# The last two gate blocks and W_out's rows move under the last memory unit, and the band attention's row sums are divided out on Pool

## The chip, the core and the metric

One core of a Trainium2 chip runs one launch of the kernel. The metric is the device time of that launch in microseconds (us), lower is better. The engines are PE (TensorE, matmuls; PEld is its weight load), DVE (VectorE), ACT (ScalarE), POOL (GpSimd) and SP, whose queue issues every DMA here.

## What is computed

One step of a one-layer encoder with 1024 prompt tokens and 8 running streams of 16 tokens, so 1152 tokens of width 1024. Cut to what matters:

```python
aq, ak, av, bq, bk, bv, mq, gate = split_projection(x, w_in, pos)   # x @ w_in, 3584 columns; b_q, b_k rotated
o_a = band_attention(aq, ak, av, a_rel_bias)     # 4 heads x 64: own chunk of 64 tokens and 8 before
o_b = diff_post(diff_attention(bq, bk, bv, lam)) # 4 heads x 128, two softmax maps
o_m = memory_attention(mq, mk, mv)               # 4 heads x 64 into 256 memory tokens
mixed = concatenate([o_a, o_b, o_m], -1)         # 1024 wide
y = (mixed * silu(gate)) @ w_out
out = layer_norm(2 ** 0.25 * x + y, ln_g, ln_b)
```

All arithmetic is in 32 bits. The new keys and values are outputs too.

## The kernel before

**Products.** An operand is split into a rounded high part and the rest (`hi`, `lo`), and a product is three matmuls, hi by hi, lo by hi, hi by lo. `w_in` is taken in 28 blocks of 128 output features; 8 of them are gate blocks, one for each 128 of the mixing width. x lies in SBUF transposed, as `xh`, `xl`, in three parts c = 0, 1, 2 of 384 tokens. `chunk` (L317 on) makes one block for one part: 8 steps over the depth of 3 matmuls each (L146 to L148), 24 matmuls of 384 columns into a `pp` tile of PSUM, of which there are two. `load_next` (L134) brings a weight block in two halves (raw tile `wraw`, two of them, L142), rounds each on ACT into `whi` (L130) and takes the difference on Pool into `wlo` (L131). Gate results go through ACT (L434) and DVE (L435) to a DRAM scratch `gates` (L436).

**Units.** The attention is done in eight units, `ORD`: M0, B0 to B3, A0, A1, M1 (two heads, or one of B). `main` is the unit's attention in small steps (scores L448 and L449, exponential, transposes L461, their split on ACT and DVE, products L663), and `merge` lays `fill` between them: the v block of the unit, gate blocks, the q block of the next unit. `NG` says how many gate blocks go with each unit; its first entry is done at the very start, part by part beside M0's q block. Results of a unit go to a DRAM scratch `mixed`.

**Band units (A).** `score` of `attention_a` takes the scores of 128 tokens against up to 640 keys, adds the bias and finds the extreme on DVE (L697), exponentiates on ACT (L703) and divides by the row sums in `normalise`: a reciprocal (L525) and a multiplication (L530), both on DVE.

**The end.** W_out has 1024 rows in 8 blocks k. `load_wout(c)` brings three of them (two for c = 2) into the room of x's part c, so it can write there only when every block has used that part. Each row block comes in two halves of 128x512 through the same two `wraw` tiles (L1084); ACT rounds each (L1085), DVE takes the rest of the first half and Pool of the second (L1086). An out step t (128 tokens) needs `mixed(t)`: gates and unit results read back (L985, L987), combined on DVE (L990, L998, L1001), split (L995 on ACT, L996 on DVE); then 48 matmuls of 512 columns over k (L1031), the residual and the layer norm. `out_steps` makes t = 0 and 1 as the fill of M1; its last step k = 7 needs the first quarter of M1's result (`closed`). Steps t = 2 to 8 follow M1 on their own, and M1's part for the running streams lies among them (its first products on PE are L790).

**Order.** A scheduler puts the instructions of each engine in order by priorities and its own time line when the kernel is built, so the written order is not the executed one. Each engine, and SP's queue, then runs strictly in that order: an instruction that waits holds all behind it.

Of the kernel before, what the change touches and what calls it, by code (L numbers as in the profile page):

```python
# [10 lines left out]
ALU = mybir.AluOpType  # L11
# [27 lines left out]
LW = 1  # L39
LEAD = 4.25  # L40
ORD = ["M0", "B0", "B1", "B2", "B3", "A0", "A1", "M1"]
NG = [1, 1, 1, 1, 1, 1, 2, 0]
GW = 2
PE = mybir.EngineType.PE
SP = mybir.EngineType.SP
# [17 lines left out]
def hybrid_step(tc, d, o):  # L63
    nc = tc.nc
# [50 lines left out]
    order = [base[names[0][0]][0] + names[0][1]]  # L115
    gates = iter(GATES)
    for i, (kind, idx) in enumerate(names):
        order += [b + idx for b in base[kind][1:]]
        late = [20 + next(gates) for _ in range(NG[i])]
        if i != 6:  # L120
            order += late
        if i < 7:
            order.append(base[names[i + 1][0]][0] + names[i + 1][1])
        if i == 6:
            order += late
    loaded = {}

    def split_half(hi, lo, raw, i, eng):
# [4 lines left out]
    def load_next(early=None):  # L133
        if len(loaded) == len(order):  # L134
            return
        blk = order[len(loaded)]
        hi = wst.tile([P, KT, P], F32R, tag="whi")
        lo = wst.tile([P, KT, P], F32R, tag="wlo")
        loaded[blk] = (hi, lo)
        for i in range(2):  # L140
            raw = early.tile([P, 4, P], F32, tag="mraw", bufs=MB) if early else wst.tile([P, 4, P], F32, tag="wraw")
            nc.sync.dma_start(raw, d["win"][blk, :, 512 * i : 512 * i + 512].rearrange("p (k c) -> p k c", c=P))  # L142
            split_half(hi, lo, raw, i, nc.gpsimd)
# [52 lines left out]
    with tc.tile_pool(name="early", bufs=1) as ep_:  # L196
        ep = Pool(ep_)
        memh = ep.tile([P, KT, 256], F32R, tag="memh")
        meml = ep.tile([P, KT, 256], F32R, tag="meml")
        wm = []  # L200

        def split_part(hi, lo, raw, a, b, eng):
            nc.scalar.copy(hi[:, a:b], raw)
            eng.tensor_tensor(out=lo[:, a:b], in0=raw, in1=f(hi[:, a:b]), op=ALU.subtract)  # L204

        def load_mem_w(blk):
            if blk < 2:
                hi, lo = [op_.tile([P, KT, P], F32R, tag=f"qa{i}", bufs=2) for i in range(2)]
            else:
                if blk == 2:  # L210
                    hi, lo = [op_.tile([P, KT, P], F32R, tag=f"ka{i}") for i in range(2)]
                else:
                    both = op_.tile([P, 2, KT, P], F32R, tag="va")
                    hi, lo = both[:, 0], both[:, 1]
            wm.append((hi, lo))
            cut = PC if blk == 0 else [0, 4, 8]
            for i, (a, b) in enumerate(zip(cut, cut[1:])):
                raw = ep.tile([P, b - a, P], F32, tag="mraw", bufs=MB)
                nc.sync.dma_start(raw, d["wmem"][blk, :, P * a : P * b].rearrange("p (k c) -> p k c", c=P))
                split_part(hi, lo, raw, a, b, nc.gpsimd if i or blk == 0 else nc.vector)  # L220
                if blk == 0:
                    memr = ep.tile([P, b - a, 256], F32, tag="xr", bufs=XB)
                    nc.sync.dma_start(memr, d["memT"][:, 256 * a : 256 * b].rearrange("p (k c) -> p k c", c=256))
                    split_part(memh, meml, memr, a, b, nc.vector)

        def load_x(c):
            for a in range(0, KT, 2):
                xr = ep.tile([P, 2, CH], F32, tag="xr", bufs=XB)
                nc.sync.dma_start(xr, d["xT"][c, :, CH * a : CH * (a + 2)].rearrange("p (k c) -> p k c", c=CH))
                split_part(xh[c], xl[c], xr, a, a + 2, nc.gpsimd if a in XP else nc.vector)  # L230

        kvs = []

        def mem_block(blk):
            ps = ps_p.tile([P, 256], F32, tag="pp")
            for k in range(KT):
                step(ps, wm[blk], memh, meml, k)
            kv = ep.tile([P, 256], F32, tag=f"memkv{blk}")
            kvs.append(kv)
            nc.vector.tensor_copy(kv, ps)  # L240


        warm = ps_t.tile([P, P], F32, tag="pt")
        for _ in range(WU):
            nc.tensor.matmul(warm, lhsT=sqzs[0][0], rhs=sqzs[0][0], start=True, stop=True)
        stores = []
        mem0 = []

        def mem_part(blk):
            mem_block(blk)  # L250
            out, scr = (o["mkT"], mkscr) if blk < 2 else (o["mvT"], mvscr)
            stores.append((out[blk % 2], kvs[blk]))
            if blk == 1:
                stores.append((mkscr, kvs[blk]))
            if blk < 2:
                return
            pt = ps_t.tile([P, 2, P], F32, tag="pt")
            for t in range(2):
                nc.tensor.transpose(pt[:, t], kvs[blk][:, t * P : (t + 1) * P], ident)
            mv = ep.tile([P, 2, P], F32, tag=f"memv{blk}")  # L260
            nc.scalar.copy(mv, pt)
            if blk == 3:
                stores.append((mvscr.rearrange("p (t e) -> p t e", t=2), mv))
            else:
                mem0.append(mv)

        with tc.manual_schedule(engines={SP}):
            for blk in range(4):
                load_mem_w(blk)
            load_next(ep)  # L270
            load_x(0)
            for blk in range(4):
                mem_part(blk)
            load_next(ep)
            load_x(1)
            load_x(2)
            for out, kv in stores:
                nc.sync.dma_start(out, kv)
            nc.sync.dma_start(cos, d["cos"])
            nc.sync.dma_start(sin, d["sin"])  # L280
        units = [setup(*n) for n in names]
        split_mem(units[0], kvs[0], mem0[0].rearrange("p t (h e) -> p t h e", h=2))
# [11 lines left out]
    for i in range(2):  # L294
        nc.vector.tensor_tensor(
            out=dl[:, i * 128 : i * 128 + 64], in0=dl[:, i * 128 : i * 128 + 64],
# [226 lines left out]
    def normalise(e, r, act):  # L523

        nc.vector.reciprocal(r, r)  # L525
        if act:
            nc.vector.tensor_scalar_mul(r, r, 0.5)
            nc.scalar.mul(e, e, r)
        else:
            nc.vector.tensor_scalar(out=e, in0=e, scalar1=r, scalar2=0.5, op0=ALU.mult, op1=ALU.mult)  # L530
# [134 lines left out]
    def attention_a(u, need):  # L665
# [3 lines left out]
        def unit(j, h):  # L669
# [14 lines left out]
            def score(i):  # L684
                kt0 = base[i]
                n = (i - kt0 + 1) * P
                b0 = 640 - n
                w_ = n if n <= 512 else n // 2
                e = pp.tile([P, 640], F32, tag="p")
                p[i] = e  # L690
                nm = small.tile([P, 2], F32, tag="nm")
                low = 3e38
                for c in range(n // w_):
                    ps = ps_s.tile([P, 512], F32, tag="ps")
                    cs = slice(c * w_, (c + 1) * w_)
                    scores(u, h, i, ps[:, 0:w_], kt0 * P + c * w_, w_)
                    nc.vector.tensor_tensor_reduce(  # L697
                        out=e[:, cs], in0=ps[:, 0:w_], in1=u.nb[:, h, b0 + c * w_ : b0 + (c + 1) * w_],
                        scale=1.0, scalar=low, op0=ALU.add, op1=ALU.min, accum_out=nm[:, c : c + 1])
                    low = nm[:, c : c + 1]  # L700
                nm = low
                rs = small.tile([P, 1], F32, tag="rs")
                nc.scalar.activation(e[:, :n], e[:, :n], AF.Exp, bias=nm, scale=-1.0, accum_out=rs)  # L703
                normalise(e[:, :n], rs, False)
                if i == 0:
                    nc.gpsimd.memset(e[:, P : 2 * P], 0.0)

# [249 lines left out]
    gates = iter(GATES)  # L957
# [166 lines left out]
    for i, u in enumerate(units):  # L1124
# [12 lines left out]
            vb, ve = [], []  # L1137
        more = []
        gs = [gate_block(next(gates)) for _ in range(NG[i] if i else 0)]
        if i != 6:  # L1140
            more += sum(sum(gs, []), [])
        if nxt:
            more += sum(q_of(nxt), [])
            fill = vb + more[:4] + ve + more[4:]
            if i == 6:

                for c in range(3):
                    for g in gs:
                        fill += g[c]
                    fill.append((0.0, lambda c=c: load_wout(c)))  # L1150
                stages = sample_of(u)
                fill = fill[:ES] + with_stages(fill[ES:], EV)
            if u.kind == "M":
                fill = with_stages(fill, 8)
        else:
            fill = out_steps(0, u) + out_steps(1, u)

        def need(kt, u=u, fill=fill):
            while u.vdone <= kt // 3:
# [105 lines left out]
```

## Time and profile before

| | us |
|---|---|
| median of 3 runs | 701.17 (700.27 to 702.02) |
| the profiled execution | 702.39, of which the span of its trace is 700.6 |
| PE busy | 669.1 (96%) |
| DVE busy | 483.8 (69%) |
| ACT busy | 354.0 (51%) |
| POOL busy | 211.9 (30%) |

A busy PE is not PE at its peak: matmuls overlap, so the distance between two starts, not the length of one, is what a matmul costs, and idle time of PE counts only waits that are longer than that overlap. A lowered clock shows as a granted clock (PEclk) under 1.00.

### The profile page before, as it was taken

What the parts mean: (1) busy time and instruction counts of PE and PEld (TensorE: products, weight loads), DVE (VectorE), ACT (ScalarE), POOL (GpSimd) and SP (SyncE); (2) the same over time, 40 slices, a digit from 0 to 9 for tenths busy, and PEclk for the clock granted to TensorE, in tenths of its full rate; (3) what the DMA queues carried; (4) which work ended last, traced back from release to release, by engine and by line L of the source; (5) the groups of instructions that cost most, each with busy time, mean ns of one, the idle gap of its engine ahead of it and who ended that gap; (6) DMA issues with size and microseconds to landing.
All of it is one profiled execution on the core that took longest, in us unless ns stands there. A gap on an engine that the chain in (4) does not pass through costs nothing.

```text
span 700.6 us, 12139 instructions
## 1 busy us (share of the span) xinstructions
PE 669.1 (96%) x4306; PEld 620.0 (88%) x4306; DVE 483.8 (69%) x1201; ACT 354.0 (51%) x922; POOL 211.9 (30%) x250
## 2 busy tenths in 40 slices
PE   8989999999999999999999999999999795999995
PEld 7989899999989999999999999999999573787884
DVE  4858766789676866798566627764785749388954
ACT  5747555457455654465455635675565654121000
POOL 7843322352235323442233222111022200224102
PEclk9999999999999999999999999999999797999998
DMA  8851342213221223133222122132236505776311
GB/s 260 304 182 52 124 132 78 53 50 106 84 72 38 97 72 84 38 99 132 87 69 68 50 91 73 40 138 72 88 109 180 171 7 186 268 270 208 139 72 61
DMA packets 55692, 78.90 MB, mean 113 GB/s; under 512 B 9368, under 2 KB 33232, under 8 KB 55632
## 3 DMA queue, kind: packets, MB, share of 16 engines
q1 hardware_dynamic: 55632, 78.13, 33.9%
q8 instruction: 34, 0.56, 0.3%
q14 instruction: 26, 0.21, 0.1%
HBM read 57.69 MB, written 20.42 MB: 111 GB/s over the span
## 4 chain that ended last, share of the span: by engine, by line
PE 83%; DMA 5%; DVE 5%; ACT 3%; POOL 1%; issue 1%; SPq 0%; POOLq 0%; ACTq 0%; DVEq 0%
PE pp L146 16%; PE pp L147 16%; PE pp L148 16%; PE pp L1031 7%; PE ps L1031 6%; PE pt L461 4%; PE po L624 4%; PE ps L449 4%; PE ps L448 4%; PE po L663 3%; DMA wraw<-in_wout 2%; DVE xl L204 1%; PE pt L875 1%; DMA p<-mixed 1%; PE ps L790 1%
## 5 line engine op out<-in xcount | busy, mean ns | idle before, releaser
L146 PE MATMUL pp<-xh,whi 128*128 128x384 f32 x672 | 229.8, 342 | 3.3 <-DVE qa L163 2.5
L148 PE MATMUL pp<-xh,wlo 128*128 128x384 f32 x672 | 228.8, 340 | 0.3 <-POOL wlo L131 0.3
L147 PE MATMUL pp<-xl,whi 128*128 128x384 f32 x672 | 228.9, 341 | 0.0
L146 PEld LDWEIGHTS pp<-xh,whi 128*128 128x128 f32 x672 | 126.5, 188 | 6.6 <-issue 2.7
L147 PEld LDWEIGHTS pp<-xl,whi 128*128 128x128 f32 x672 | 126.5, 188 | 2.7 <-POOL xl L204 0.4
L148 PEld LDWEIGHTS pp<-xh,wlo 128*128 128x128 f32 x672 | 126.4, 188 | 1.8 <-POOL wlo L131 0.6
L131 POOL TENSOR_TENSOR wlo<-wraw,whi 128x512 fp32r<-128x512 f32 x52 | 70.5, 1376 | 110.7 <-ACT whi L130 104.0
L590 ACT ACTIVATE p<-ps,nm 128x512 f32<-128x512 f32 (+3 forms) x96 | 55.3, 580 | 39.8 <-DVE nm L587 26.5
L448 PE MATMUL ps<-ka,qa 128*128 128x512 f32 (+4 forms) x176 | 59.3, 343 | 4.7 <-ACT p L752 4.1
L461 PE MATMUL pt<-ident,p 128*128 128x128 f32 x332 | 56.0, 281 | 2.4 <-DVE ptl L465 1.0
L449 PE MATMUL ps<-kl,qa 128*128 128x512 f32 (+4 forms) x176 | 57.7, 331 | 0.0
L585 DVE TENSOR_REDUCE nm<-ps 128x1 f32<-128x512 f32 (+3 forms) x96 | 51.3, 549 | 7.1 <-PE ps L449 5.5
L465 DVE TENSOR_TENSOR ptl<-pt,pth 128x512 fp32r<-128x512 f32 x56 | 38.3, 686 | 15.5 <-ACT pth L464 15.3
L461 PEld LDWEIGHTS pt<-ident,p 128*128 128x128 f32 x332 | 40.6, 144 | 5.9 <-DVE ptl L465 1.4
L464 ACT CAST pth<-pt 128x512 fp32r<-128x512 f32 x56 | 32.9, 587 | 17.8 <-PE pt L461 15.3
L1031 PE MATMUL pp<-xh,whi 128*128 128x512 f32 (+1 forms) x96 | 38.0, 395 | 3.1 <-ACT whi L995 3.1
L448 PEld LDWEIGHTS ps<-ka,qa 128*128 128x128 f32 x176 | 33.7, 192 | 6.9 <-ACT p L752 5.5
L1031 PE MATMUL pp<-xl,whi 128*128 128x512 f32 (+1 forms) x96 | 37.3, 388 | 0.0
L1031 PE MATMUL pp<-xh,wlo 128*128 128x512 f32 (+1 forms) x96 | 36.4, 385 | 0.0
L624 PE MATMUL po<-pth,va 128*128 128x256 f32 (+1 forms) x160 | 35.0, 282 | 0.0
L449 PEld LDWEIGHTS ps<-kl,qa 128*128 128x128 f32 x176 | 33.9, 193 | 0.3
L161 POOL TENSOR_TENSOR qa<-t,qa 64x384 fp32r<-64x384 f32 (+1 forms) x24 | 22.0, 918 | 38.1 <-ACT qa L159 37.1
(223 smaller groups left out, 1322.2 us busy)
## 6 DMA issues: line engine op xcount, KB each, us to landing
wraw<-in_win SPq DMA_DIRECT2D x52, 256.0 KB, 2.8
xr<-in_xT SPq DMA_DIRECT2D x12, 384.0 KB, 5.8
gates<-t SPq DMA_DIRECT2D x24, 192.0 KB, 2.7
qa<-in_xn SPq DMA_DIRECT2D x9, 512.0 KB, 3.5
wraw<-in_wout SPq DMA_DIRECT2D x16, 256.0 KB, 4.4
p<-gates SPq DMA_DIRECT2D x8, 512.0 KB, 5.7
out_y<-qa SPq DMA_DIRECT2D x16, 256.0 KB, 2.0
mixed<-od SPq DMA_DIRECT2D x28, 128.0 KB, 1.8
```

What stands on the lines that cost most here:

```text
L131: eng.tensor_tensor(out=lo[:, h], in0=raw, in1=f(hi[:, h]), op=ALU.subtract)
L146: nc.tensor.matmul(ps, lhsT=w[0][:, k], rhs=xh_[:, k], start=(k == 0), stop=False)
L147: nc.tensor.matmul(ps, lhsT=w[0][:, k], rhs=xl_[:, k], start=False, stop=False)
L148: nc.tensor.matmul(ps, lhsT=w[1][:, k], rhs=xh_[:, k], start=False, stop=(k == KT - 1))
L448: nc.tensor.matmul(ps, lhsT=u.qa[h][:, qs], rhs=u.ka[h][:, k0 : k0 + n], start=True, stop=False)
L449: nc.tensor.matmul(ps, lhsT=u.qa[h][:, qs], rhs=kl[h][:, k0 : k0 + n], start=False, stop=True)
L461: nc.tensor.transpose(pt[:, t, q * P : (q + 1) * P], p[q][:, cols[t][q] : cols[t][q] + P], ident)
L465: nc.vector.tensor_tensor(out=lo, in0=pt, in1=f(hi), op=ALU.subtract)
L585: nc.vector.tensor_reduce(out=nm[:, m, c : c + 1], in_=ps[c][:, : b - a], axis=AX.X, op=ALU.max, negate=True)
L590: nc.scalar.activation(e[:, a:b], ps[c][:, : b - a], AF.Exp, bias=nm[:, m, 0:1], accum_out=rs[:, m, c : c + 1])
L624: nc.tensor.matmul(out, lhsT=a, rhs=b, start=(g == 0 and x == 0), stop=(g == j and x == len(mm) - 1))
L1031: nc.tensor.matmul(y, lhsT=a[:, k], rhs=b[k][:, s], start=(k == 0 and x == 0), stop=(k == KT - 1 and x == 2))
```

## The change

It has two parts. **First**, `NG` is shifted by one unit: no gate block is done at the start, each unit from B0 to A1 takes one, and M1 takes two. With it goes the second early weight load: the block after M0's q is now loaded behind all of x. The last two gate blocks are written part by part (block, block, then W_out's rows of that part) as the fill of M1, ahead of the two out steps; before they were in this form the fill of A1. **Second**, in `attention_a` the multiplication by the reciprocal goes from DVE to Pool, with the same operands.

```diff
-NG = [1, 1, 1, 1, 1, 1, 2, 0]
+NG = [0, 1, 1, 1, 1, 1, 1, 2]
...
-        late = [20 + next(gates) for _ in range(NG[i])]
-        if i != 6:
-            order += late
+        order += [20 + next(gates) for _ in range(NG[i])]
...
-            load_next(ep)
             load_x(1)
             load_x(2)
+            load_next()
...
-                normalise(e[:, :n], rs, False)
+                nc.vector.reciprocal(rs, rs)
+                nc.gpsimd.tensor_scalar(out=e[:, :n], in0=e[:, :n], scalar1=rs, scalar2=0.5, op0=ALU.mult, op1=ALU.mult)
...
-        if i != 6:
+        if nxt:
             more += sum(sum(gs, []), [])
...
-                for c in range(3):
-                    for g in gs:
-                        fill += g[c]
-                    fill.append((0.0, lambda c=c: load_wout(c)))
...
         else:
-            fill = out_steps(0, u) + out_steps(1, u)
+            fill = []
+            for c in range(3):
+                for g in gs:
+                    fill += g[c]
+                fill.append((0.0, lambda c=c: load_wout(c)))
+            fill += out_steps(0, u) + out_steps(1, u)
```

What the scheduler makes of it shows at three places. On PE, at the last matmuls of the last gate block (`pp_9049`), before, and the first of out step 0 (`pp_9163`): between them stand A1's last transposes (`pt`) and products (`po_8473`), and scores (`ps`) of M1.

```order
L147 MATMUL pp_9049<-xl_28_124,whi_8121 128x384
L148 MATMUL pp_9049<-xh_27_123,wlo_8122 128x384
L663 MATMUL po_8473<-ptl_8597,va_7966 64x128
L461 MATMUL pt_8680<-ident_81,p_8397 128x128
...
L449 MATMUL ps_9198<-kl_21_112,qa_1279_8283 128x256
L663 MATMUL po_8473<-pth_8618,va_7966 128x256
...
L461 MATMUL pt_8812<-ident_81,p_8563 128x128
...
L449 MATMUL ps_9225<-kl_22_113,qa_1280_8284 128x256
L1031 MATMUL pp_9163<-xh_1350_8745,whi_9153 128x512
```

The same place in the change (`pp_9243` is the last gate tile, `pp_9358` that of out step 0; L144 and L1028 are L148 and L1031 of before):

```order
L143 MATMUL pp_9243<-xl_28_124,whi_8466 128x384
L144 MATMUL pp_9243<-xh_27_123,wlo_8467 128x384
L444 MATMUL ps_9306<-ka_1374_8746,qa_1357_8577 128x256
L445 MATMUL ps_9306<-kl_21_112,qa_1357_8577 128x256
L444 MATMUL ps_9314<-ka_1375_8747,qa_1358_8578 128x256
L445 MATMUL ps_9314<-kl_22_113,qa_1358_8578 128x256
L1028 MATMUL pp_9358<-xh_1403_8930,whi_9348 128x512
```

Four score matmuls are left between the gates and the out step; the rest of A1 and most scores of M1 now stand among the gates. Behind the last gate and up to L790 there were 32 scores, 56 transposes, 65 products and 97 matmuls of L1031, and are now 8, 24, 32 and 97.

On SP, at the first loads: before, the second weight block (`mraw_352`, `mraw_356`) stood ahead of x's part 1, and the third (`wraw_443`) among it.

```order
L229 DMA xr_228<-in_xT 128x768
L142 DMA mraw_352<-in_win 128x512
L142 DMA mraw_356<-in_win 128x512
L229 DMA xr_360<-in_xT 128x768
L229 DMA xr_364<-in_xT 128x768
L142 DMA wraw_443<-in_win 128x512
L142 DMA wraw_447<-in_win 128x512
```

Now all of x comes first, and one block (B0's q) behind it:

```order
L229 DMA xr_370<-in_xT 128x768
L229 DMA xr_374<-in_xT 128x768
L229 DMA xr_378<-in_xT 128x768
L138 DMA wraw_384<-in_win 128x512
L138 DMA wraw_388<-in_win 128x512
```

Two weight loads have left the stretch in which x arrives, and with them two of Pool's L131 there.

On Pool, in A1, the multiplications (L701) stand in one queue with the weights' L131 (here L127); the rows are those of the change, before there was nothing of the band attention between the weights' rows.

```order
L127 TENSOR_TENSOR wlo_7987<-wraw_7988,whi_7986 128x512
L127 TENSOR_TENSOR wlo_7987<-wraw_7992,whi_7986 128x512
L701 TENSOR_SCALAR p_8172<-p_8172,rs_8182 128x640
L701 TENSOR_SCALAR p_8237<-p_8237,rs_8247 128x640
L701 TENSOR_SCALAR p_8303<-p_8303,rs_8313 128x640
L701 TENSOR_SCALAR p_8388<-p_8388,rs_8398 128x640
L127 TENSOR_TENSOR wlo_8467<-wraw_8468,whi_8466 128x512
L127 TENSOR_TENSOR wlo_8467<-wraw_8472,whi_8466 128x512
L701 TENSOR_SCALAR p_8452<-p_8452,rs_8462 128x640
L701 TENSOR_SCALAR p_8532<-p_8532,rs_8542 128x640
```

The last two multiplications of A1 are queued behind the rest of the last gate's weights.

## Rows read from the trace of the kernel before

**Rows 1.** The profile page: PE's busy tenths by slice; a DMA's landing.

```profile
PE   8989999999999999999999999999999795999995
wraw<-in_wout SPq DMA_DIRECT2D x16, 256.0 KB, 4.4
```

**Rows 2.** Stretches, 543.7 to 692.7: length, busy of five engines (instructions), granted clock, DMA share, GB/s.

```profile
543.70:554.80 11.10, 6.38 (x30) 5.05 (x28) 8.78 (x23) 7.86 (x21) 2.54 (x2) 0.74 0.63 199
554.80:582.00 27.20, 24.78 (x134) 20.47 (x134) 15.40 (x47) 13.84 (x38) 1.28 (x1) 0.92 0.10 31
582.00:593.00 11.00, 4.08 (x15) 2.34 (x14) 10.18 (x30) 5.92 (x18) 0.92 (x1) 0.71 0.68 243
593.00:608.30 15.30, 15.30 (x68) 12.73 (x68) 6.75 (x13) 3.31 (x5) 2.12 (x1) 0.87 0.80 282
608.30:612.20 3.90, 2.35 (x38) 1.30 (x36) 1.95 (x3) 0.00 (x0) 1.41 (x1) 1.00 0.59 213
612.20:692.70 80.50, 80.50 (x432) 65.57 (x428) 60.89 (x97) 8.96 (x16) 18.78 (x13) 1.00 0.46 158
```

**Rows 3.** Timeline of PE: start us, us, operation, idle before and its releaser.

```profile
543.29 0.33 PE L148 MATMUL pp<-xh,wlo 128*128 128x384 f32 x1
...
554.80 0.80 PE L1031 MATMUL pp<-xh,whi 128*128 128x512 f32 x1 [1.04 <-ACT whi L995]
...
592.97 0.80 PE L1031 MATMUL pp<-xh,whi 128*128 128x512 f32 x1 [2.06 <-ACT whi L995]
```

**Rows 4.** Timeline of PE: spacing of gate matmuls, of transposes, of scores.

```profile
537.72 0.34 PE L148 MATMUL pp<-xh,wlo 128*128 128x384 f32 x1
...
538.41 0.34 PE L146 MATMUL pp<-xh,whi 128*128 128x384 f32 x1
...
543.52 0.60 PE L461 MATMUL pt<-ident,p 128*128 128x128 f32 x4
543.88 0.36 PE L448 MATMUL ps<-ka,qa 128*128 128x256 f32 x1
544.08 0.28 PE L449 MATMUL ps<-kl,qa 128*128 128x256 f32 x1
...
544.55 0.28 PE L449 MATMUL ps<-kl,qa 128*128 128x256 f32 x1
```

**Rows 5.** Chain that ended last, by time: a W_out half's transfer, an out step's matmuls.

```profile
528.42 3.47 DMA wraw<-in_wout
...
617.85 5.62 PE pp L1031 x24
```

**Rows 6.** Timeline of the start, 19 to 39 us: PE, DVE and Pool splitting x.

```profile
38.84 0.41 PE L146 MATMUL pp<-xh,whi 128*128 128x384 f32 x1 [2.45 <-DVE qa L163]
...
19.27 0.95 DVE L204 TENSOR_TENSOR xl<-xr,xh 128x768 fp32r<-128x768 f32 x1
...
30.18 6.82 DVE L204 TENSOR_TENSOR xl<-xr,xh 128x768 fp32r<-128x768 f32 x3 [0.30 <-ACT xh L203]
...
29.30 9.37 POOL L204 TENSOR_TENSOR xl<-xr,xh 128x768 fp32r<-128x768 f32 x4
```

**Rows 7.** Timeline of ACT: first and last cast of W_out.

```profile
519.00 1.14 ACT L1085 CAST xh<-wraw 128x512 fp32r<-128x512 f32 x2
...
557.72 0.62 ACT L1085 CAST xh<-wraw 128x512 fp32r<-128x512 f32 x1 [1.25 <-DMA wraw<-in_wout]
```

**Rows 8.** Groups by line and shape: busy us, mean ns, idle before and releaser.

```profile
L530 DVE TENSOR_SCALAR p<-p,rs 128x640 f32<-128x640 f32 x16 | 10.8, 675 | 0.5
...
L131 POOL TENSOR_TENSOR wlo<-wraw,whi 128x512 fp32r<-128x512 f32 x52 | 70.5, 1376 | 110.7 <-ACT whi L130 104.0 <-PE pt L461 6.0 <-POOL qa L161 0.4
...
L105 POOL MEMSET pz<- 128x1024 f32 x1 | 1.0, 951 | 0.0
...
L1086 POOL TENSOR_TENSOR xl<-wraw,xh 128x512 fp32r<-128x512 f32 x8 | 10.8, 1346 | 36.3 <-ACT xh L1085 36.3
```

**Rows 9.** Stretches of A0 and A1, 393 to 545 us, summed: length, busy of engines.

```profile
sum 152.00, PE 150.31 PEld 145.14 DVE 94.85 ACT 85.39 POOL 28.66; mean PE 18.79 PEld 18.14 DVE 11.86 ACT 10.67 POOL 3.58
```

More of the change, by code (lines that the diff above doesn't have):

```diff
@@ L118, in hybrid_step @@
         order += [b + idx for b in base[kind][1:]]
-        late = [20 + next(gates) for _ in range(NG[i])]
-        if i != 6:
-            order += late
+        order += [20 + next(gates) for _ in range(NG[i])]
         if i < 7:
             order.append(base[names[i + 1][0]][0] + names[i + 1][1])
-        if i == 6:
-            order += late
     loaded = {}
```

## Prediction, written before the change was run

> **What bounds the kernel now.** First the page's slices: PE is full except in its first two and in slices 32 to 35, about 543 to 612 us [rows 1]. So the time is PE's work plus what PE loses at the start, in that stretch and in the tail. Next the stretch itself, cut where PE's work changes [rows 2, 3]. The last gate matmul starts at 543.29. Out step 0 could begin then, but its first matmul starts at 554.80, and what ended PE's wait there is ACT's split of `mixed` (L995). Between 543.70 and 554.80 PE is busy 6.38 of 11.10 us at a granted clock of 0.74. Step 0 and M1's matmuls take until 582.00 at 0.92; then a second hole follows, 4.08 busy of 11.00 at 0.71, until step 1 starts at 592.97, again released by L995; step 1 runs at 0.87; 3.9 us more pass to 612.20. From there PE is full, 80.50 of 80.50.
>
> How much of these 68.7 us is work? I price matmuls by the distance between starts at full clock [rows 4]: 384 columns 0.69/4 = 0.1725 us, a transpose 0.36/4 = 0.09, a score or a product of 256 columns 0.47/4 = 0.1175; 512 columns 5.62/24 = 0.234 [rows 5]. Behind the last gate up to L790 stand 97 L1031 (22.7 us), 32 scores (3.8), 56 transposes (5.0), 54 products of 256 columns (6.3), 11 narrow ones and 16 small matmuls (about 1.6 together): 39.4 us. So 68.7 - 39.4 = 29.3 us are lost there. By place: the first hole holds 3.3 of this work and loses about 8; step 0's stretch (20.2 of work in 27.2) loses 7; the second hole (1.4 of work) 9.6; step 1 (13.3 in 15.3, the clock) 2; the end 2.7.
>
> Why the first hole: W_out's casts stand in ACT's queue from 519.00 to 557.72, and the late ones wait for their DMA [rows 7]; L995 stands behind some of them. A half takes 4.4 us from issue to landing by the page [rows 1] and 3.47 in the chain [rows 5], with two raw tiles for 16 halves. So **the late stage is paced by transfers and by a chain over DVE and ACT**, and PE has too little other work there.
>
> **The change, part by part.** *Gates under M1.* No gate matmul is removed: 8 blocks of 72 before and after. In the late stage the order of PE now has 8 scores, 24 transposes and 32 products behind the last gate. So 24 x 0.1175 + about 22 x 0.1175 + 32 x 0.09 = 8.3 us of work, with narrow matmuls about 9.3, moved from behind the gates to among them; 30.1 us remain behind. The gates (two blocks, 144 x 0.1725 = 24.8 us) now lie beside M1's attention and W_out's loads. When the first third of both blocks is done, 96 gate matmuls (16.6 us) and some 7.7 us of others still follow: W_out's loads start about 24 us of PE work before the last gate, as before (519.0 against 543.3). What is new is that those 24 us cover M1's first steps and the readbacks for step 0.
>
> What stays lost, estimated place by place. Under the gates 3.5 us (0 to 8): ACT's in-order queue stands at W_out's casts while M1's exponentials and transposes' splits queue behind, and DVE stands at L998 until the gates are read back; PE waits for both once its two `pp` tiles are full. Step 0: 2 (0 to 6). The hole between the steps: 9 (3 to 13), because `mixed` for step 1 is still loaded behind W_out's last loads on SP, and its chain L990, L998, L995, L996 is unchanged. Step 1's clock: 1.8 (0 to 4). The end: 0.3. Sum 16.6 against 29.3: **12.7 us gained**. The last W_out cast would come at about 553.3 - 27.8 + 38.7 = 564.2, where 553.3 is the end of the gates in the new count, 27.8 is 24.3 of work and 3.5 of stalls, and 38.7 the length of the casts' train [rows 7]. By queue positions I get 568 to 570 when L995 and the gates' writes are put between. Step 0 wants its last block (k = 7) at about 569: nearly a tie, so the train is the first rival below.
>
> *The start.* One block, 72 x 0.1725 = 12.4 us of PE work, leaves the start and is done later; its sum is the same, so only cover is lost. It filled PE while x was split, three parts on DVE in 6.82 us and four on Pool in 9.37, to 38.67; PE then waited only 2.45 us for a `pp` tile that L163 frees behind those splits [rows 6]. Against it: one weight load and its two L131 (2 x 1.376 = 2.75 us on Pool, [rows 8]) leave that stretch, so x should be complete near 36 instead of 38.7, and M0's q blocks and B0's weights follow closely (near 37). PE then waits before 37 rather than at 38.8, with 12.4 us less to do. I count a gain of 1.5, between a gain of 2.5 (about all of that time) and a loss of 2.5 (a wait like the 2.45 once more).
>
> *The multiplication on Pool.* 32 tiles, 16 of them 640 wide; their 10.8 us at 0.675 leave DVE [rows 8]. In A0 and A1 DVE is busy 94.85 of 152.00 and PE 150.31 [rows 9], so DVE's relief there gives PE nothing. On Pool the operation isn't in the trace: by the MEMSET of 1024 columns (0.951) 640 cost 0.59, by the two-input L131 of 512 (1.376) 1.72. I take 0.75, near the first, since only one tensor is read. Pool is busy 28.66 of 152.00 [rows 9], so even 32 x 1.72 = 55 us would fit. Between a tile's last score and its first transpose stand at least 12 us of PE rows in the changed order, typically 15 to 28, which cover the exponential, the reciprocal and Pool's turn. Price on the path: 0. If that cover is gone, each delay beyond it is PE's own wait.
>
> The one-input price has a rule beside it. The Trainium skill (GPSIMD Engine Reference, section 4.1, Engine selection) says that one-input elementwise work runs at about line rate on GpSimd and two-input work some 2 times slower than on VectorE. By it an estimate would be VectorE's 0.675 per tile; for two inputs the rows agree in direction only (L204 took 0.95 alone on DVE and 2.34 on Pool, beside each other). The sum would not move by either.
>
> Sum: 702.39 - 12.7 - 1.5 + 0 = 688.2 for a profiled execution like the one shown; that one lies 1.2 above the median, so **687.0** at medians.
>
> **The rivals.** *R1, W_out's train ends last (0.13).* If a half costs 4.4 from issue to landing instead of 3.47 over the 8 rounds of two tiles, the train is 7.4 us longer, and the gates' writes and `mixed` loads between on SP add about 2. Step 0 then stands at its late k by some 9.5 us: 696.5. For it: the late casts already wait for their DMA [rows 7]. Against: L1085's wait there is 1.25, not more.
>
> *R2, the hole between the steps closes too (0.13).* With `mixed` for step 1 read before the train's end, 8 of its 9 us are gone: 679. For it: M1's attention is further ahead by then and DVE freer. Against: L995 ended that wait [rows 3], and the order ahead of it is unchanged.
>
> *R3, Pool becomes the bound in the band units (0.06).* This one ends slower. Pool's order is strict, and a multiplication stands behind pairs of L131 that wait for ACT's casts: 104 of their 110.7 us of idle time [rows 8]; also a DVE operation with two inputs slows beside Pool, L204 0.95 alone and 2.27 beside it [rows 6]. Sixteen pairs in the two units, each two rows longer by about 1.04 (1.72 against 0.675), fully exposed, cost 33 us: 702.39 - 14.2 + 33 - 1.2 = 720. It decides as soon as the delay from exponential to transposes exceeds the 12 us of cover; above 14.2 us exposed the kernel is slower than before. Against it: L131's waits fall mostly where no band tile is pending, and Pool has 123 idle us [rows 9].
>
> On R3's second half: the Trainium skill (SBUF — State Buffer, section SBUF: two separate sides) says that VectorE and GpSimd share one port pair, which an operation holds for its whole length as an exclusive lock when VectorE reads two SBUF inputs and GpSimd reads SBUF. The 0.95 against 2.27 agrees; by it the new Pool rows would hold up DVE's two-input rows, by at most their own 0.75 each.
>
> *R4, nothing gained (0.05).* The gates only push the stage back: M1's steps and the readbacks don't run ahead, because DVE and ACT are held in order, and the 29.3 us come back behind them: 701, give or take 2. This is also the case that the change doesn't do what it says. For it: in step 0's stretch DVE has 15.40 and ACT 13.84 of 27.20 [rows 2], so waits, not work, hold them, and waits can move along.
>
> **How the numbers follow.** Forecast 687 (its bounds 683 to 693 by the terms above taken two at a time): 0.63; R1 696.5: 0.13; R2 679: 0.13; R4 701: 0.05; R3 720: 0.06. The range reaches from R2's side to R1's, 677 to 697, leaving out R3, R4 and the outer ends. A measurement of this kernel can tell about 0.3%, 2.1 us, from no change: faster means under 699.1. Faster 0.63 + 0.13 + 0.13 = 0.89, same 0.05, slower 0.06.
>
> **What would show it.** Right: the first L1031 within about 1 us of the last gate; step 0's stretch near 19 us instead of 27; the granted clock at 1.00 up to step 0's end; a hole of 9 to 11 us still before step 1, ended by L995; the full stretch that began at 612.20 beginning at 597 to 599, and 80.5 long as before; band units at PE 150 of 152; Pool's multiplication near 0.75. Wrong: a wait of PE for transposed band tiles with Pool as the releaser (R3); L1031 late in step 0 waiting for W_out's casts (R1); no second hole (R2); PE idle among the gates for ACT or DVE by more than 8 us (R4); a start longer by more than 2.5 us.

## The result, and the profile of the changed kernel

| | before | changed |
|---|---|---|
| median (4 runs each) | 701.6 us | 685.62 us (684.38 to 685.8) |
| ratio to before | | 0.977 (0.975 to 0.979) |
| the profiled execution | 702.39, span 700.6 | 685.8, span 684.0 |
| last gate matmul starts | 543.29 [rows 3] | 553.45 |
| first matmul of out step 0 | 554.80 [rows 3] | 554.09 |
| first matmul of out step 1 | 592.97 [rows 3] | 577.26 |
| PE full from | 612.20 [rows 2] | 595.60 |

Timed once more beside some of the experiments, the changed kernel took 686.83, ratio 0.979 (0.976 to 0.981). The forecast was 687.0 in a range of 677 to 697.

The page's two slices of PE (first its busy tenths, then the granted clock), which answer to [rows 1]: the two weak slices, the 7 and the 5 there, have become one, a 6, and one lowered place of the clock is left in the body.

```profile
PE   8899999999999999999999999999999996999995
...
PEclk9999999999999999999999999999999998899999
```

The stretches that answer to [rows 2] (length, busy of PE, PEld, DVE, ACT, POOL with instructions, granted clock, DMA share, GB/s). From the last rows of the gates to out step 0, step 0, the hole, step 1, and the full rest:

```profile
535.00:553.62 18.62, 18.59 (x126) 17.70 (x124) 13.42 (x36) 12.87 (x35) 5.15 (x4) 1.00 0.50 165
553.62:572.00 18.38, 17.71 (x100) 14.76 (x100) 12.75 (x34) 12.34 (x30) 3.88 (x3) 1.00 0.64 225
572.00:577.26 5.26, 0.72 (x7) 0.48 (x5) 4.89 (x10) 2.89 (x5) 0.00 (x0) 0.82 0.62 186
577.26:594.50 17.24, 15.88 (x57) 12.58 (x57) 11.23 (x19) 1.67 (x3) 5.22 (x3) 0.76 0.81 292
595.60:675.00 79.40, 79.40 (x424) 64.65 (x421) 58.27 (x93) 7.32 (x14) 17.68 (x12) 1.00 0.44 153
```

PE's timeline at the same places as [rows 3] (start, us, operation, idle before and its releaser). The first hole is gone: out step 0 starts 0.64 us after the last gate matmul. The second is there, shorter, and ACT's split of `mixed` (L992, L995 of before) ends it again:

```profile
553.45 0.34 PE L144 MATMUL pp<-xh,wlo 128*128 128x384 f32 x1
...
554.09 0.39 PE L1028 MATMUL pp<-xh,whi 128*128 128x512 f32 x1
...
577.26 0.79 PE L1028 MATMUL pp<-xh,whi 128*128 128x512 f32 x1 [4.54 <-ACT whi L992]
...
582.40 1.22 PE L1028 MATMUL pp<-xh,wlo 128*128 128x512 f32 x2 [1.36 <-DVE rs L1051]
```

The books close on PE alone. The last gate matmul starts 10.2 us later (543.29 to 553.45), the stretch from there until PE is full shrinks by 26.8, from 68.9 to 42.1 us, and what follows is 88.4 us long in both (700.6 - 612.2 and 684.0 - 595.6). 10.2 - 26.8 = -16.6, which is the difference of the spans.

### The profile page after: what moved, and what is told of

It reads as the page before. It is cut to its first block, busy times and chain, and to the rows that moved or that the text cites. A ratio compares the mean times of both kernels' runs of the same rounds, so it can differ in the third digit from the quotient of the medians.

```text
span 684.0 us, 12210 instructions
## 1 busy us (share of the span) xinstructions
PE 662.8 (97%) x4306; PEld 614.2 (90%) x4306; DVE 472.6 (69%) x1169; ACT 356.3 (52%) x922; POOL 233.5 (34%) x282
## 5 line engine op out<-in xcount | busy, mean ns | idle before, releaser
L144 PE MATMUL pp<-xh,wlo 128*128 128x384 f32 x672 | 228.9, 341 | 0.0
L144 PEld LDWEIGHTS pp<-xh,wlo 128*128 128x128 f32 x672 | 126.4, 188 | 1.7 <-issue 0.2
L127 POOL TENSOR_TENSOR wlo<-wraw,whi 128x512 fp32r<-128x512 f32 x54 | 72.4, 1361 | 66.1 <-ACT whi L126 50.9
L701 POOL TENSOR_SCALAR p<-p,rs 128x640 f32<-128x640 f32 (+4 forms) x32 | 21.5, 676 | 64.3 <-DVE rs L700 58.7
L1028 PE MATMUL pp<-xh,whi 128*128 128x512 f32 (+1 forms) x96 | 37.5, 392 | 4.5 <-ACT whi L992 4.5
L1028 PE MATMUL pp<-xh,wlo 128*128 128x512 f32 (+1 forms) x96 | 37.0, 387 | 1.4 <-DVE rs L1051 1.4
L1028 PE MATMUL pp<-xl,whi 128*128 128x512 f32 (+1 forms) x96 | 37.1, 386 | 0.0
L992 ACT CAST whi<-p 128x1024 fp32r<-128x1024 f32 (+2 forms) x9 | 8.6, 954 | 53.5 <-PE pp L1028 42.9
L465 DVE TENSOR_TENSOR ptl<-pt,pth 128x256 fp32r<-128x256 f32 (+1 forms) x72 | 25.2, 352 | 15.8 <-ACT pth L464 15.2
```

The source lines that it names most:

```text
L127: eng.tensor_tensor(out=lo[:, h], in0=raw, in1=f(hi[:, h]), op=ALU.subtract)
L144: nc.tensor.matmul(ps, lhsT=w[1][:, k], rhs=xh_[:, k], start=False, stop=(k == KT - 1))
L1028: nc.tensor.matmul(y, lhsT=a[:, k], rhs=b[k][:, s], start=(k == 0 and x == 0), stop=(k == KT - 1 and x == 2))
```

## Experiments

The kernel before ran beside each set; ratios and intervals are to it. "Last gate to full PE" is the stretch of the profiled execution from the start of the last gate matmul to the first L1031 (L1028 of the change) behind the last L790, where PE is full for good. Runs that are not in the table are told in the text.

| run | gate blocks at start / under A1 / under M1 | median | ratio | last gate to full PE |
|---|---|---|---|---|
| before | 1 / 2 / 0 | 701.6 | 1 | 68.9 |
| e1_pool_only | 1 / 2 / 0 | 701.25 | 0.999 (0.996 to 1.002) | 65.0 |
| e11_three_a1 | 0 / 3 / 0 | 693.92 | 0.989 (0.986 to 0.992) | 55.0 |
| e6_one_gate | 0 / 2 / 1 | 693.52 | 0.989 (0.986 to 0.992) | 50.5 |
| e4_block_by_block | 0 / 1 / 2 | 698.5 | 0.995 (0.993 to 0.997) | 54.6 |
| e2_gates_only | 0 / 1 / 2 | 689.75 | 0.982 (0.979 to 0.985) | 49.1 |
| changed | 0 / 1 / 2 | 685.62, 686.83 | 0.977, 0.979 | 42.1, 43.0 |
| e7_three_gates | 0 / 0 / 3 | 680.64 | 0.969 (0.966 to 0.972) | 37.4 |

**The two parts apart.** In e1 only the multiplication moves:

```diff
-                normalise(e[:, :n], rs, False)
+                nc.vector.reciprocal(rs, rs)
+                nc.gpsimd.tensor_scalar(out=e[:, :n], in0=e[:, :n], scalar1=rs, scalar2=0.5, op0=ALU.mult, op1=ALU.mult)
```

> The kernel before with the second part of the change alone: in the band units the multiplication by the reciprocal goes to Pool, and the gate blocks stay where they were. Theory T (all of the gain comes from the gate blocks that now cover the last memory unit; the multiplication is hidden on either engine): 701.6, give or take 1.5. Rival P (DVE's relief of 10 us and more in the two band units reaches the path): 699 or less. Rival L (Pool's queue or the ports that Pool shares hold up the band units): 704 or more, with PE's busy time in the band units under its 150 of 152 us.

701.25, no difference that can be told. By itself the move to Pool is worth nothing. In e2 these lines of the changed kernel are put back:

> The changed kernel with the multiplication back on DVE: the first part of the change alone. Theory T: as the changed kernel, 685.6, give or take 1.5. Rival P: 688 or more, since DVE, with some 20 us more to do beside A1 and the gates, falls behind in the late stage.

689.75: the gate blocks carry most of the gain. Whether they carry all of it stays open, since the intervals of 0.982 and of the changed kernel's 0.977 and 0.979 touch. The scheduler, which knows DVE's load, leaves more of M1 behind the last gate in e2: on PE 36 transposes and 43 products there, against 24 and 32 with the multiplication on Pool, 12 x 0.09 + 11 x 0.1175 = 2.4 us by the prices of [rows 4]. To see whether it is DVE's load, e8 gives that load back (a multiplication by 1.0) with Pool's in place:

```diff
+                nc.vector.tensor_scalar(out=e[:, :n], in0=e[:, :n], scalar1=1.0, scalar2=1.0, op0=ALU.mult, op1=ALU.mult)
                 nc.vector.reciprocal(rs, rs)
```

> The changed kernel with one more multiplication on DVE (by 1.0, the same size) ahead of Pool's in each band tile, so DVE has the load that it had before the change, and Pool its own too. It asks why the changed kernel without the move to Pool took 689.8. Theory T' (DVE's time in A1 and under the gates decides how much of M1 gets ahead of the last gate: the order on PE then leaves 36 transposes and 43 products behind it instead of 24 and 32, as in that run): 689 to 691. Rival O (it is the chain from exponential to transposes, not DVE's load): 685 to 687.

687.31, ratio 0.980 (0.977 to 0.983), between the two theories. Behind the last gate stood as many transposes and products on PE as in e2 (36 and 43), so DVE's load does set how much of M1 is left there; but the time lies between e2 and the changed kernel and can be told from neither. That the move to Pool helps a little once the gates are late is possible and not settled.

**The cover of a band tile.** e9 adds four more multiplications by 1.0 on Pool behind each one:

```diff
                 nc.gpsimd.tensor_scalar(out=e[:, :n], in0=e[:, :n], scalar1=rs, scalar2=0.5, op0=ALU.mult, op1=ALU.mult)
+                nc.gpsimd.tensor_scalar(out=e[:, :n], in0=e[:, :n], scalar1=1.0, scalar2=1.0, op0=ALU.mult, op1=ALU.mult)
...
```

> The changed kernel with four more multiplications (by 1.0, the same size) on Pool behind the one in each band tile: about 3.3 us more for each tile of 640 columns, some 85 us on Pool in all. It prices the cover that a band tile has between its scores and its transposes. Theory T (at least 12 us of PE's work lie between, so this costs nothing): 685.6, give or take 1.5. Rival L (Pool's queue or the ports that it shares with DVE hold up the units): 690 or more, by 0.3 us or more for each of the 16 wide tiles.

682.25, ratio 0.973 (0.971 to 0.976): not slower; by the ratios some 2 to 4 us faster than the changed kernel, though the intervals touch. The stretches of e9, the first the two band units as in [rows 9], then step 0, the hole, step 1:

```profile
393.00:545.00 152.00, 150.97 (x1061) 145.03 (x1059) 92.41 (x270) 87.95 (x228) 114.89 (x171) 1.00 0.31 97
554.28:569.20 14.92, 14.92 (x86) 12.75 (x85) 10.66 (x27) 10.07 (x24) 3.90 (x3) 1.00 0.57 174
569.20:575.76 6.56, 3.35 (x21) 2.38 (x19) 6.09 (x11) 3.92 (x8) 1.29 (x1) 1.00 1.00 374
575.76:590.40 14.64, 14.56 (x61) 11.09 (x61) 12.45 (x22) 2.46 (x4) 5.21 (x3) 0.88 0.89 315
```

Pool is busy 114.89 of 152 and PE still 150.97, so the cover is real and the Pool rival is out. The gain looks like a side effect: the scheduler, given other loads, ordered DVE differently at the hole. In the changed kernel two halves of step 0's residual and its statistics (L1035, L1036) stand ahead of the combination for step 1 (L995), in e9 one half does (L1039; L999 is L995):

```profile
572.71 0.68 DVE L1035 SCALAR_TENSOR_TENSOR qa<-qa,pp 128x512 f32<-128x512 f32 x1
573.30 0.74 DVE L987 SCALAR_TENSOR_TENSOR p<-p,subg,rs 128x512 f32<-128x512 f32 x1
573.97 0.68 DVE L1035 SCALAR_TENSOR_TENSOR qa<-qa,pp 128x512 f32<-128x512 f32 x1
574.57 0.68 DVE L1036 BATCH_NORM_STATS2 st<-qa 128x6 f32<-128x512 f32 x1
575.17 1.07 DVE L995 TENSOR_TENSOR p<-p,p 128x896 f32<-128x896 f32 x1
```

```profile
572.39 0.75 DVE L991 SCALAR_TENSOR_TENSOR p<-p,subg,rs 128x512 f32<-128x512 f32 x1
573.05 0.68 DVE L1039 SCALAR_TENSOR_TENSOR qa<-qa,pp 128x512 f32<-128x512 f32 x1
573.65 1.08 DVE L999 TENSOR_TENSOR p<-p,p 128x896 f32<-128x896 f32 x1
```

L995 starts 1.5 us earlier there, PE's wait is 2.54 instead of 4.54, and step 1 runs at a clock of 0.88 instead of 0.76. No run changes this order alone, so the cause is read from the traces, not shown. But if the order is worth 3 us or so, smaller differences between versions of this kernel carry little.

**The start.** e3 keeps one block there (and its early weight load) and takes it from B0:

```diff
-NG = [0, 1, 1, 1, 1, 1, 1, 2]
+NG = [1, 0, 1, 1, 1, 1, 1, 2]
...
+            load_next(ep)
             load_x(1)
             load_x(2)
-            load_next()
```

> The changed kernel with one gate block at the start as before (and the second early weight load with it), none under B0 instead; two still under M1. It prices the start by itself. Theory T (the block at the start cost about 1.2 us of waits there, by the 13.4 us that B0's first scores moved forward against 12.4 us of matmuls taken out): 686.8. Rival S (the start is neutral, what was won there was lost in B0): 685.6, within 0.5. Rival U (the block at the start was good cover, and the change lost something there): 684.5 or less.

689.68, ratio 0.982 (0.979 to 0.985), later than all three. PE's first score of 512 columns in the B units and the second in A0, of the changed kernel and of e3:

```profile
89.47 0.39 PE L444 MATMUL ps<-ka,qa 128*128 128x512 f32 x1
...
395.44 0.39 PE L444 MATMUL ps<-ka,qa 128*128 128x512 f32 x1
```

```profile
102.17 0.40 PE L444 MATMUL ps<-ka,qa 128*128 128x512 f32 x1
...
398.68 0.39 PE L444 MATMUL ps<-ka,qa 128*128 128x512 f32 x1
```

The first pair, 12.70 us apart, does not price the start: ahead of that score e3 has not only the block's 72 matmuls more, but 76 of 384 columns and 32 small ones. The same holds for the 13.4 us that theory T started from. At the second pair both have done the same rows, and e3 is 3.24 us behind. Where they went shows in PE's busy time, between B0's first score of 512 columns and one in B1 ahead of which both have again done the same rows (the changed kernel, then e3):

```profile
89.47:214.08 124.61, 124.61 (x826) 120.07 (x826) 91.18 (x235) 68.20 (x188) 46.24 (x58) 1.00 0.25 77
```

```profile
102.17:217.81 115.64, 112.40 (x719) 106.14 (x718) 88.96 (x232) 65.72 (x185) 43.15 (x57) 1.00 0.22 67
```

PE of e3 is idle for 3.24 us there, nearly all of it in four waits between 157.00 and 182.91, and that of the changed kernel never. So the 3 us were lost in B0 and B1, the first of which had no gate block to fill its waits, and next to nothing at the start. No theory had that: T looked for the cost at the start, and S and U expected no longer time. What e3 shows is that B0 without a block pays about 3 us.

**The place of the blocks.** e11 takes the start's block and the multiplication as the change does, but leaves all late blocks under A1 (the first whole, two part by part):

```diff
-NG = [1, 1, 1, 1, 1, 1, 2, 0]
+NG = [0, 1, 1, 1, 1, 1, 3, 0]
...
+        else:
+            more += sum(gs.pop(0), [])
```

> The block taken from the start and the multiplication on Pool, as in the change, but the late blocks all under A1 (the first whole, the last two part by part with W_out's rows behind), none under M1. It takes the place under M1 alone out of the change. Theory T (the gain is the cover under M1): 698 to 702, with the two holes and the two lowered stretches of the clock as before. Rival S (a good part of the gain is the shorter start, or the part on Pool): 690 to 696.

693.92. My theory falls here: 8 of the 16 us come without a single block under M1. Its order tells why: behind the last gate stand 32 transposes and 36 products, where before there were 56 and 65. M1 alone has 32 of each, so only 4 of A1's products are left: the third block lets A1's remainder get done among the gates. What is left is M1, and it shows in PE's waits:

```profile
577.40 0.58 PE L447 MATMUL ps<-ka,qa 128*128 128x256 f32 x1 [4.34 <-ACT p L752]
...
584.19 0.79 PE L1031 MATMUL pp<-xh,whi 128*128 128x512 f32 x1 [1.20 <-ACT whi L995]
```

e6 moves one of these three under M1, e7 all three (the first whole):

```diff
-NG = [0, 1, 1, 1, 1, 1, 1, 2]
+NG = [0, 1, 1, 1, 1, 1, 2, 1]
```

> The changed kernel with one gate block under M1 and two under A1 (none at the start): half the cover, and W_out's loads start with some 8 us of gate matmuls left. Theory T (M1's work needs cover, and the loads need to start some 17 us of gate matmuls ahead of the end; the run with block by block showed 698.5 with two blocks and the late start): 697 to 702. Rival A (the gain is in proportion to the gate work under M1): half of the 16 us, 693 to 695.

```diff
-NG = [0, 1, 1, 1, 1, 1, 1, 2]
+NG = [0, 1, 1, 1, 1, 1, 0, 3]
...
+            fill += sum(gs.pop(0), [])
             for c in range(3):
```

> The changed kernel with three gate blocks under M1 (the first whole, the last two part by part) and none under A1. Theory T (two blocks cover what can be covered: the hole between the steps waits for a load, not for cover; and A1 loses its block, as B0 did in the run with the start kept, where that cost 2.9 us): 686 to 690. Rival A (in proportion to the gate work under M1, as the run with one block went: 8 us for a block): 678 to 681.

693.52 and 680.64: both fell in rival A's range, e6 by coincidence, since e11 takes as long without any block under M1. e7 is the fastest version of the study, 6 us under the changed kernel on the same chip. The stretches of e7 (M1's rest and step 0, where the hole was, step 1):

```profile
551.18:569.00 17.82, 15.47 (x87) 13.00 (x87) 12.76 (x37) 13.08 (x34) 4.57 (x4) 1.00 0.65 217
569.00:576.30 7.30, 6.11 (x36) 4.41 (x35) 7.07 (x13) 4.38 (x8) 0.00 (x0) 1.00 0.62 164
576.30:587.40 11.10, 11.10 (x52) 8.85 (x50) 10.25 (x19) 1.91 (x3) 4.23 (x3) 1.00 0.98 368
```

PE is 6.11 of 7.30 busy where the changed kernel had 0.72 of 5.26, and the clock stays at 1.00 in all three stretches. In A1, without a block, PE lost nothing to speak of: from A0's second score of 512 columns (394.41) to the last gate matmul (551.01) it is busy 156.12 of 156.60 us. So what B0 paid without a block, A1 did not.

**The loads' early start.** e4 has the two blocks under M1 one after the other, with W_out's rows behind the parts of the second:

```diff
+            fill += sum(gs[0], [])
             for c in range(3):
-                for g in gs:
-                    fill += g[c]
+                fill += gs[1][c]
                 fill.append((0.0, lambda c=c: load_wout(c)))
```

> The changed kernel with the two last gate blocks one after the other under M1, not part by part: W_out's rows stand behind the parts of the second block, so W_out's loads can begin only with some 8 us of gate matmuls left instead of 17. Theory T (the loads' train of 39 us is the thing that must start early; it ends about when step 0 wants its last row block, so it has hardly any slack): the train ends 8 us later and the time is 5 to 8 us longer, 691 to 694, with waits of PE for W_out's casts in step 0. Rival H (the train is hidden, only the amount of gate work under M1 counts): 685.6 to 687.5.

698.5: 13 of the 16 us are gone. First and last cast of W_out on ACT, of the changed kernel, then of e4:

```profile
528.56 1.13 ACT L1082 CAST xh<-wraw 128x512 fp32r<-128x512 f32 x2
...
565.53 0.62 ACT L1082 CAST xh<-wraw 128x512 fp32r<-128x512 f32 x1 [0.82 <-DMA wraw<-in_wout]
```

```profile
541.20 1.13 ACT L1082 CAST xh<-wraw 128x512 fp32r<-128x512 f32 x2
...
591.51 0.62 ACT L1082 CAST xh<-wraw 128x512 fp32r<-128x512 f32 x1 [4.52 <-DMA wraw<-in_wout]
```

And PE's longest wait in e4:

```profile
586.40 1.44 PE L1028 MATMUL pp<-xh,whi 128*128 128x512 f32 x2 [6.95 <-ACT xh L1082]
```

The train starts 12.6 us later (I had said 8) and needs 50.9 us instead of 37.6, because other loads of the out steps come among it on SP. The last cast is 26 us later, and the theory's sign was right, its size half of what happened. In e6 too the casts begin late (540.97) and end late (587.25), and PE waits 8.1 us in all for W_out's splits (L1082, L1083), against 0.5 in e11, whose casts run from 525.41 to 565.47. So the late loads take back what one block under M1 brings.

**The hole between the steps.** e5 gives step 1's loads tiles of their own, free earlier, and asks for them ahead of W_out's last two row blocks:

```diff
+                if c == 2:
+                    fill.append((0.0, lambda: start(1)))
                 fill.append((0.0, lambda c=c: load_wout(c)))
```

> The changed kernel, with what out step 1 reads (its gates and the units' results) given tiles of its own that come free early (the room of the last band unit's q) and asked for ahead of W_out's last two row blocks, not behind all of them. Theory T (the hole of 7.7 us between the steps, of which 1.9 are work, is the wait for this load behind W_out, and the 10.2 us of half clock after it follow from the idle hole): the wait of 4.5 us for L992 is gone, the half clock with it, 676 to 681. Rival M (the step then waits for M1's own results or for DVE, as the 1.4 us for L1051 show): 682 to 685. Rival W (the loads push W_out's train back): 686 or more.

682.26, ratio 0.973 (0.971 to 0.976), rival M's size by another way. The hole and its lowered clock are gone. But DVE and ACT now split step 1's operand first and step 0's after it, and the first matmul of step 0 comes at 558.99, 4.8 us after the last gate matmul (554.19), not 0.64:

```profile
552.46 1.08 DVE L993 TENSOR_TENSOR wlo<-qa,whi 128x896 fp32r<-128x896 f32 x1
...
558.97 1.09 DVE L993 TENSOR_TENSOR wlo<-kc,whi 128x896 fp32r<-128x896 f32 x1 [0.27 <-ACT whi L992]
```

```profile
558.99 0.50 PE L1028 MATMUL pp<-xh,whi 128*128 128x512 f32 x1 [0.33 <-ACT whi L992]
```

Its two stretches run at full clock; part of the wait has moved ahead of step 0. e10 joins this with the three blocks of e7:

> Three gate blocks under M1 together with the early load for step 1 (682.3 with two blocks). Theory T: the third block under M1 adds no cover and A1 loses its own, so 682 to 686. Rival A: with the wait for the load gone, the remaining 5 us lost between the last gate and M1's end want cover, so 677 to 680.

684.01, ratio 0.974 (0.971 to 0.977): slower than e7 alone. With three blocks the hole is filled anyway, and what is left is the late step 0: its first matmul comes at 559.98, 6.0 us after the last gate matmul. It costs a second time, since the granted clock is 0.83 in that gap and 0.84 from 560 to 575, where PE is busy throughout. And the changed kernel once more:

> The changed kernel itself once more, on the chip of the next three, since the other versions lie within a few us of each other and their chips differ. It was 685.6 there; 684.5 to 687 here if the chips agree. By the ratio to the kernel before, 0.975 to 0.979. The run of the first part alone was at 0.982: if this one comes out at 0.981 or more, the part on Pool has brought nothing that can be told.

686.83, ratio 0.979: the first result again. Against e2's 0.982 that leaves the part on Pool where e8 left it.

## Why the prediction held, point by point

**The total** was right within 1.4 us, in part by luck: step 0 and the hole were priced 4.1 us too high, step 1 and the end behind it 2.8 too low.

**The start**: 1.5 us were forecast. The two traces show 1.2, which can't be told from nothing. A0's second score of 512 columns, ahead of which both kernels have done the same rows but for the block, moved from 409.09 to 395.44 (shown above), 13.65 us for 12.42 of matmuls; before it stood here:

```profile
409.09 0.40 PE L448 MATMUL ps<-ka,qa 128*128 128x512 f32 x1
```

But PE's first matmul on x starts at 20.07 in the changed kernel's trace and at 21.75 before, and x's first part is loaded ahead of all that the change moves. In the eleven traces with the changed kernel's order at the start this first matmul comes anywhere from 19.96 to 22.62, and B0's first score of 512 columns from 88.68 to 91.06.

The wait of 2.45 for L163 [rows 6] fell to 0.22, as said; but PE now waits for x itself, in PE's timeline of the changed kernel:

```profile
22.51 0.44 PE L143 MATMUL pp<-xl,whi 128*128 128x384 f32 x1 [0.76 <-POOL xl L200]
...
27.81 0.44 PE L143 MATMUL pp<-xl,whi 128*128 128x384 f32 x1 [1.65 <-DVE xl L200]
...
36.82 0.42 PE L142 MATMUL pp<-xh,whi 128*128 128x384 f32 x1 [0.22 <-DVE qa L159]
```

**Under the gates**: 3.5 us of loss were forecast, about 2 came by the same count, and hardly any as a wait: PE was busy 18.59 of 18.62 us before the last gate's end. In-order ACT and DVE did not hold it up. By the forecast's terms the next matmul would have started at 543.5 - 1.5 + 9.3 + 3.5 = 554.8; it started at 553.6, with 1.2 us won at the start, so 2.0 were lost or the 9.3 us of moved work were priced too low. The 553.3 that the prediction has for this point, and with it its 564.2 for W_out's last cast, is 1.5 less than its own terms give.

**Step 0**: 2 us of loss forecast. Its stretch has PE busy 17.71 of 18.38, at full clock, as forecast, and the 0.67 that is missing are the first two waits of the hole. W_out's last cast, forecast for 564 or for 568 to 570, came at 565.53, and no matmul of step 0 waited for one. R1 was rightly small for this order; in e4, with the loads later, the same mechanism decides.

**The hole between the steps**: 9 us forecast, 5.2 came (the waits of 0.39, 0.28 and 4.54), the last ended by L992 as said, and not at zero as R2 had it. Step 0 and the hole together take 23.6 us (553.62 to 577.26) for 16.7 of work, the 30.1 behind the gates less the 13.4 of step 1, so 6.9 were lost where 2 and 9 were forecast.

**Step 1** is where the loss was under-priced: 1.8 us for the lowered clock, 0.3 for the end, and nothing for other waits. From the hole's end until PE is full 18.3 us pass for 13.4 of work by the forecast's prices (49 L1028, 8 products, 1.0 for the small ones), so 4.9 were lost. The clock is at 0.76 in 577.26 to 594.50: until 585.6 PE does 3.5 us of work in 8.3, of which 1.36 is a wait and the other 3.4 the half clock. The wait of 1.36 is put down to L1051, but the real one is the row of DVE just ahead of it, L993, which took 2.54 us for 896 columns where e5's took 1.08 (below).

Behind the last gate's end the sum is 42.0 - 30.1 = 11.9 us of loss, forecast 13.1.

**The multiplication on Pool**: 0.815 us measured for 640 columns, 0.75 forecast between 0.59 and 1.72. Its price on the path was put at 0; e1 finds no difference, and e9 shows that the cover holds. What the forecast left out is that DVE's relief changes the order that the scheduler writes; e2 and e8 show it in the order, not yet in the time.

**The mechanism**: the forecast had 9.3 us of other work moved in among the gates, and that is what the runs bear out, but it spoke of M1's first steps and the readbacks. e11 shows that about half of the gain is A1's remainder, done among the gates because a third block is late at all, wherever it stands.

## What to carry to other kernels

Where a last stage waits for transfers and for a chain over other engines, hold back some independent matmul work for it, and count which rows still stand behind the last of it: the 68.9 us behind the last gate became 55.0 with a third late block under A1, and 42.1 and 37.4 with two and three of the three under M1. Place the work so that the loads that depend on it can start early, since the same blocks in a whole-block order lost 13 us. And when a hole is closed by asking for its data earlier, look at whose turn that takes on the in-order engines, as e5 and e10 show.

## What the runs showed of the hardware

**A DVE row with two inputs in SBUF waits for a whole Pool row.** In the changed kernel's step 1 (Pool's row, then DVE's):

```profile
579.31 2.09 POOL L995 TENSOR_TENSOR p<-p,p 128x896 f32<-128x896 f32 x1 [11.79 <-DVE p L987]
```

```profile
579.81 2.54 DVE L993 TENSOR_TENSOR wlo<-p,whi 128x896 fp32r<-128x896 f32 x1
```

Pool's row ends at 581.40, DVE's at 582.35, 0.95 later, and the same row takes 1.08 alone. That it stood still until Pool was done, and did not only run slower beside it, shows in rows of 768 columns at the start, which take 0.96 alone. Those that begin 0.36, 1.17 and 1.76 us before Pool's row ends take 1.18, 1.98 and 2.58, and all three end 0.81 to 0.82 us after it. The last of them (Pool's row, then DVE's):

```profile
24.93 2.02 POOL L200 TENSOR_TENSOR xl<-xr,xh 128x768 fp32r<-128x768 f32 x1
```

```profile
25.18 2.58 DVE L200 TENSOR_TENSOR xl<-xr,xh 128x768 fp32r<-128x768 f32 x1
```

The Trainium skill (SBUF — State Buffer, section SBUF: two separate sides) calls the pair of ports that the two share an exclusive lock held for the whole instruction; this trace agrees, in step 1 on PE's path, and the prediction, which cited it for the band units, had not looked for it here.

**Pool's price by size.** From 128 to 640 columns the multiplication took (mean)

```profile
L701 POOL TENSOR_SCALAR p<-p,rs 128x640 f32<-128x640 f32 x16 | 13.0, 815 | 36.3 <-DVE rs L700 31.9 <-PE pt L408 2.3 <-PE pp L144 2.0
...
L701 POOL TENSOR_SCALAR p<-p,rs 128x128 f32<-128x128 f32 x4 | 1.5, 376 | 10.4 <-DVE rs L700 10.4
```

(815 - 376)/512 = 0.86 ns a column and some 266 ns besides, against 675 ns for 640 columns on DVE [rows 8].

**The clock lags the wait.** Slices of 1 us in the changed kernel (granted clock third from the end): PE has been idle since 573, the clock falls from 2.4 to 1.2 GHz after 575, stays there under step 1's first matmuls and is back after 585, though PE had work from 577.26. So a hole of 5 us cost a second time, in the work behind it.

```profile
574.00:575.00 1.00, 0.00 (x0) 0.00 (x0) 1.00 (x3) 0.17 (x1) 0.00 (x0) 1.00 0.05 22
575.00:576.00 1.00, 0.00 (x0) 0.00 (x0) 1.00 (x2) 0.00 (x0) 0.00 (x0) 0.69 0.55 160
576.00:577.00 1.00, 0.00 (x0) 0.00 (x0) 1.00 (x4) 0.72 (x1) 0.00 (x0) 0.50 0.98 141
584.00:585.00 1.00, 1.00 (x4) 0.81 (x3) 0.95 (x3) 0.00 (x0) 0.00 (x0) 0.50 1.00 325
585.00:586.00 1.00, 1.00 (x4) 0.76 (x4) 1.00 (x3) 0.00 (x0) 0.00 (x0) 0.69 0.94 362
586.00:587.00 1.00, 1.00 (x6) 0.77 (x5) 1.00 (x2) 0.00 (x0) 0.00 (x0) 1.00 0.89 348
```
